# One decoder layer: the loads of the sample's cached sliding keys and values move from SyncE's queue to GpSimd's

## The chip, the cores and the metric

The kernel runs on one core of one Trainium2 chip, as one launch. The metric is the device time of that launch in microseconds (us), the median of several runs. Before the change it is 3061.63 us (three runs, 3060.77 to 3061.79).

TensorE (PE) multiplies matrices; its weight loads (PEld) are listed beside it. VectorE (DVE), ScalarE (ACT) and GpSimd (POOL) do elementwise work, and SyncE (SP) does none: it issues DMAs. Each engine takes its own instructions strictly in the order in which the program lists them, and an instruction waits for its semaphores with everything behind it.

## The reference, cut to what matters

One layer of a decoder trunk is computed for a prompt of 512 tokens and for a sample group of 8 sequences of 8 new tokens each, in float32. All 576 tokens share the weights. Four mixers (a gated delta rule, a state-space scan, a dilated sliding-window attention and a gated linear recurrence) feed one output projection, then follow cross-attention over 256 memory tokens and a convolved gated FFN.

The change touches only the sliding-window attention of the sample group. There each sequence has 2048 cached rows of keys and values, 8 heads of 64 channels:

```
k_ext = concatenate([k_buf, k_new], axis=1)          # v_ext likewise
for dist, bias in ((128, 1), (512, 4), (2048, 16)):  # (window, dilation)
    kg, vg = k_ext[:, lb + loc - dist], v_ext[:, lb + loc - dist]
    e = exp(q . kg * scale + bias - max);  out = sum(e * vg) / sum(e)
```

The 512 newest cached rows serve all three dilations. Of the 1536 older ones, only every sixteenth is read for a given query.

## The kernel before, in words

PE runs the projections as three passes (high by high, low by high, high by low halves) over weight blocks of 512 KB. `block` (L119) loads such a block into `raw` through SP; ACT and DVE split it into `hi` and `lo`; `linear` (L151) multiplies. All loads and stores of the program are issued by SP.

Nobody writes the order of an engine's instructions by hand. The program is traced with priorities, and a planner plays it forward in planned time, giving each engine its most urgent ready instruction; this fixes each engine's list. `at` sets the level: weights before drains, then "mix" (the delta rule among others), then "side", and "fill" last, at which `linear`'s matmuls are traced. The sample's attention is "side", called by `sample_step` from the callbacks of three projections: `swa_kv` (L856ff), `lru` and `delta_z`, while the delta rule (`delta`, L1411ff) is interleaved as "mix".

`sample_step` calls four parts, all of which the change touches through their loads:

- `old_keys(t0)`, for 8 query positions: six tiles of 128 rows by 512 (8 sequences, 16 old rows of each), loaded by `old` (L952), multiplied by the query (L967, four of six on POOL and two on DVE), and summed by head on DVE (L968).
- `old_values(t0)`: six such tiles of values (L952), weighted (L1012, again four of six on POOL) and added up on DVE (L1014).
- `sample_keys(pr, hp)`, 16 calls: two loads of 512 newest keys by 128 channels (L1054: each partition gets four runs of 512 bytes), which PE transposes (L1057); ACT or DVE copies the result, and PE forms the logits (L1063).
- `sample_values(pr)`, 4 calls: eight loads of 128 rows of values (L1095, 2 KB in each partition), which PE multiplies with the weights (L1100).

All of these loads are of 256 KB, and their tiles share four buffers (`tag="kn", bufs=4`). A load therefore waits until the tile four before it has been read for the last time. That last reader is POOL or DVE for an old tile, and PE for the newest keys and values.

POOL has other work in the same stretch: for the delta rule L1492, L1502, L1504, L1557, L1608, L1613 and L1636, and small copies at L869, L1070, L1298 and L1299. SP's queue holds, besides, the weight blocks (L119), the delta rule's inputs `dw<-dn` (L1459) and its sample states `dw<-in_state_delta` (L1606).

Of the kernel before, what the change touches and what calls it, by code (L numbers as in the profile page):

```python
# [284 lines left out]
class Post(Net):  # L285
    def add_x(self, g=None, first=False, out=False):

        nc = self.nc
        if g:
            self.xh, self.xl = {}, {}  # L290
            for k in range(15, -1, -1):
                self.xh[k], self.xl[k] = (self.xn[k // 4].tile([128, NT], F32R, name=f"x{z}{k}") for z in "hl")

        def done(m, ps):
            x = self.xT[:, m]
            with self.at("evac"):
                old = x
                if first:
                    old = self.nt()
                    nc.sync.dma_start(old, self.xd[m])  # L300
                nc.vector.tensor_tensor(x, ps, old, op=OP.add)  # L301
            if out:
                nc.sync.dma_start(self.xd[m], x)
            if g:
                nc.scalar.activation(self.xh[m], x, AF.Copy, scale=self.v(g, m))
                nc.vector.scalar_tensor_tensor(self.xl[m], x, self.v(g, m), self.xh[m], op0=OP.mult, op1=OP.subtract)
                if not out:
                    self.square(m)
        return done
# [484 lines left out]
class Swa(Post):  # L794
# [152 lines left out]
    def old(self, pool, name, k, t0):  # L947

        t = pool.tile([128, 512], F32, name="old", tag="kn", bufs=4)
        src = self.a[name]  # L950
        off = src[0, 0, 256 * k + t0, 0, 0:1].offset
        self.nc.sync.dma_start(t, bass.AP(tensor=src.tensor, offset=off, ap=[[2048 * 512, 8], [16 * 512, 16], [1, 512]]))  # L952
        return t

    def old_open(self, pool):
# [90 lines left out]
    def sample_keys(self, pr, hp):  # L1046

        nc, pool = self.nc, self.ok
        if hp == 0:
            self.S = pool.tile([128, 576], F32, name="S")  # L1050
        kt = []
        for b in (2 * pr, 2 * pr + 1):
            kn = pool.tile([128, 512], F32, name="kn", tag="kn", bufs=4).rearrange("p (j c) -> p j c", j=4)
            nc.sync.dma_start(kn, self.last("cache_win_k", b)[:, :, 128 * hp:128 * hp + 128])  # L1054
            p = self.pm()
            for j in range(4):
                nc.tensor.transpose(p[:, 128 * j:128 * j + 128], kn[:, j], self.ident)  # L1057
            kt.append(pool.tile([128, 512], F32, name="kt", tag="ow", bufs=2))
            (nc.scalar.copy if b % 2 else nc.vector.tensor_copy)(kt[-1], p)
        r = slice(32 * hp, 32 * hp + 32)  # L1060
        L = self.pm()
        for b2 in range(2):
            nc.tensor.matmul(L[r], self.Qm[:, hp, 2 * pr + b2], kt[b2], start=b2 == 0, stop=b2 == 1, skip_group_check=True)  # L1063
        nc.vector.tensor_tensor(self.S[r, :512], L[r], self.sb[r], op=OP.add)

    def sample_values(self, pr):

        nc, pool, S = self.nc, self.ok, self.S
        selh, sel2 = self.sel[:, :2], self.sel[:, 58:186].rearrange("p (g a b) -> p g a b", g=4, a=2)
        nc.gpsimd.tensor_copy(S[:, 512:], self.new[:, pr])  # L1070
        m, s = (pool.tile([128, 1], F32, name=f"sm{z}", bufs=2) for z in "ms")
        w = self.w4[:, pr:pr + 1]
        mo, so = self.mrow[:, 0, pr:pr + 1], self.mrow[:, 1, pr:pr + 1]
        nc.vector.tensor_reduce(m, S, axis=AX.X, op=OP.max, negate=True)
        nc.vector.tensor_tensor(m, m, mo, op=OP.min)
        nc.scalar.activation(S, S, AF.Exp, bias=m, accum_out=s)
        nc.scalar.activation(w, mo, AF.Exp, bias=m, scale=-1.0)
        nc.vector.scalar_tensor_tensor(s, so, w, s, op0=OP.mult, op1=OP.add)
        nc.vector.reciprocal(s, s)
        nc.vector.tensor_tensor(w, w, s, op=OP.mult)  # L1080
        pt = pool.tile([128, 512], F32, name="pt", tag="ow", bufs=2)
        p = self.pm()
        for j in range(4):
            nc.tensor.transpose(p[:, 128 * j:128 * j + 128], S[:, 128 * j:128 * j + 128], self.ident)
        nc.vector.tensor_copy(pt, p)
        p = self.pm()
        nc.tensor.transpose(p[:64, :128], S[:, 512:], self.ident)
        pn = S[:64, 256:384]
        nc.scalar.copy(pn, p[:64, :128])
        O = self.pm()  # L1090
        for b2 in range(2):
            for j in range(5):
                if j < 4:
                    v = pool.tile([128, 512], F32, name="v", tag="kn", bufs=4)
                    nc.sync.dma_start(v, self.last("cache_win_v", 2 * pr + b2)[:, j])  # L1095
                for hp in range(4):
                    c = slice(128 * hp, 128 * hp + 128)
                    r = slice(32 * hp, 32 * hp + 32)
                    lhs, rhs = (pt[:, 128 * j + 32 * hp:128 * j + 32 * hp + 32], v[:, c]) if j < 4 else (pn[:, r], self.vns[:, c])
                    nc.tensor.matmul(O[r, 128 * b2:128 * b2 + 128], lhs, rhs, start=j == 0, stop=j == 4, skip_group_check=True)  # L1100
        om = S[:, :256].rearrange("p (a e d) -> p a e d", a=2, e=2)
        for b2 in range(2):
            nc.vector.scalar_tensor_tensor(om[:, b2], O[:, 128 * b2:128 * b2 + 128].rearrange("p (e d) -> p e d", e=2), s,
                                           selh.unsqueeze(2).to_broadcast([128, 2, 64]), op0=OP.mult, op1=OP.mult)
        p = self.pm()
        for hp in range(4):
            for b2 in range(2):
                nc.tensor.matmul(p[:, 16 * hp:16 * hp + 16], om[:, b2].rearrange("p e d -> p (e d)"), sel2[:, hp, b2],
                                 start=hp == 0 and b2 == 0, stop=b2 == 1, skip_group_check=True)

        nc.vector.tensor_copy(self.kTs[:, :, 16 * pr:16 * pr + 16], p[:, :64].rearrange("p (a b) -> p a b", a=4))
# [1081 lines left out]
```

## Time and profile before

| | us |
|---|---|
| median of three runs | 3061.63 |
| the profiled execution's own time | 3060.31 |
| its span, first to last instruction | 3058.2 |
| PE busy | 2906.6 (95%) |
| DVE busy | 2083.6 (68%) |
| ACT busy | 1129.0 (37%) |
| POOL busy | 1098.4 (36%) |

The profiled execution lies 1.32 us under the median, and 2.1 us of it lie outside the span. DMA-issuing instructions are not counted as busy, so SP has no row. The first of the touched loads is issued 397.8 us after the start, the last one 991.4 us after it. The stretch from 380 to 1000 us is what the rows below mostly show.

### The profile page before, as it was taken

What the parts mean: (1) busy time and instruction counts of PE and PEld (TensorE: products, weight loads), DVE (VectorE), ACT (ScalarE), POOL (GpSimd) and SP (SyncE); (2) the same over time, 40 slices, a digit from 0 to 9 for tenths busy, and PEclk for the clock granted to TensorE, in tenths of its full rate; (3) what the DMA queues carried; (4) which work ended last, traced back from release to release, by engine and by line L of the source; (5) the groups of instructions that cost most, each with busy time, mean ns of one, the idle gap of its engine ahead of it and who ended that gap; (6) DMA issues with size and microseconds to landing.
All of it is one profiled execution on the core that took longest, in us unless ns stands there. A gap on an engine that the chain in (4) does not pass through costs nothing. (4 is left out here: it accounts for less than half of the span.)

```text
span 3058.2 us, 53977 instructions
## 1 busy us (share of the span) xinstructions
PE 2906.6 (95%) x21347; PEld 2743.7 (90%) x21347; DVE 2083.6 (68%) x3431; ACT 1129.0 (37%) x2013; POOL 1098.4 (36%) x1202
## 2 busy tenths in 40 slices
PE   8988988998999999998899999999999999999998
PEld 8888987887878879987889999999999999999996
DVE  7857756779567575648788888888888853333334
ACT  4433331353423353325344444444444432212214
POOL 4211422313112100102468889888888810000000
PEclk9999999999999999999999999999999999999999
DMA  5465566545576474244323333333333353333322
GB/s 169 133 192 152 163 181 187 166 130 163 166 209 181 136 216 143 68 127 151 118 88 110 107 102 109 107 103 110 106 100 105 113 201 114 101 97 114 107 90 104
DMA packets 370133, 408.41 MB, mean 134 GB/s; under 512 B 37718, under 2 KB 300715, under 8 KB 369176
## 3 DMA queue, kind: packets, MB, share of 16 engines
q1 hardware_dynamic: 369880, 404.96, 43.0%
q8 instruction: 168, 2.75, 0.4%
q14 instruction: 85, 0.70, 0.1%
HBM read 342.85 MB, written 64.69 MB: 133 GB/s over the span
## 5 line engine op out<-in xcount | busy, mean ns | idle before, releaser
L123 ACT CAST hi<-raw 128x1024 fp32r<-128x1024 f32 x158 | 165.6, 1048 | 489.9 <-PE acc L151 425.3
L151 PE MATMUL acc<-xh,hi 128*128 128x288 f32 x1408 | 319.3, 306 | 20.8 <-DVE nt L1192 13.8
L124 DVE TENSOR_TENSOR lo<-raw,hi 128x1024 fp32r<-128x1024 f32 x158 | 195.8, 1240 | 192.0 <-ACT hi L123 186.5
L151 PE MATMUL acc<-xh,lo 128*128 128x288 f32 x1408 | 317.8, 304 | 3.2 <-DVE lo L129 3.1
L151 PE MATMUL acc<-xl,hi 128*128 128x288 f32 x1408 | 317.5, 303 | 2.5 <-DVE xl L245 2.5
L344 DVE TENSOR_TENSOR lo<-S,hi 128x1024 fp32r<-128x1024 f32 x164 | 228.9, 1396 | 89.7 <-ACT hi L343 89.7
L151 PE MATMUL acc<-hh,hi 128*128 128x288 f32 x1280 | 276.1, 297 | 2.8 <-DVE xT L301 2.3
L151 PE MATMUL acc<-hh,lo 128*128 128x288 f32 x1280 | 274.3, 296 | 1.1 <-DVE lo L124 1.1
L151 PE MATMUL acc<-hl,hi 128*128 128x288 f32 x1280 | 275.0, 296 | 0.0
L344 DVE TENSOR_TENSOR al<-raw,ah 128x512 fp32r<-128x512 f32 x328 | 265.1, 844 | 14.2 <-ACT ah L343 14.1
L151 PEld LDWEIGHTS acc<-xh,hi 128*128 128x128 f32 x1408 | 231.8, 192 | 33.9 <-issue 26.6
L343 ACT CAST hi<-S 128x1024 fp32r<-128x1024 f32 x164 | 171.8, 1048 | 211.7 <-POOL S L539 176.9
L151 PEld LDWEIGHTS acc<-xl,hi 128*128 128x128 f32 x1408 | 232.7, 192 | 10.7 <-issue 7.4
L151 PEld LDWEIGHTS acc<-xh,lo 128*128 128x128 f32 x1408 | 231.6, 192 | 10.1 <-issue 4.6
L301 DVE TENSOR_TENSOR xT<-acc,xT 128x576 f32<-128x576 f32 x160 | 120.6, 755 | 168.3 <-PE acc L151 167.0
L536 POOL TENSOR_TENSOR S<-raw 128x256 f32<-128x256 f32 x164 | 168.8, 1029 | 154.5 <-DMA raw<-in_w_up 117.9
L128 ACT ACTIVATE hi<-raw,gmix 128x256 fp32r<-128x256 f32 x320 | 136.5, 498 | 212.8 <-PE acc L151 175.1
L151 PEld LDWEIGHTS acc<-hh,hi 128*128 128x128 f32 x1280 | 206.7, 189 | 3.6 <-ACT hi L123 2.2
L151 PEld LDWEIGHTS acc<-hh,lo 128*128 128x128 f32 x1280 | 207.0, 189 | 1.3 <-DVE lo L124 1.3
L151 PEld LDWEIGHTS acc<-hl,hi 128*128 128x128 f32 x1280 | 207.3, 189 | 0.0
L560 PE MATMUL acc<-Bh,ah 128*128 128x288 f32 x656 | 197.3, 301 | 10.3 <-ACT t L565 10.1
L634 DVE SCALAR_TENSOR_TENSOR y<-ub,vec,y 128x592 f32<-128x592 f32 x176 | 179.9, 1042 | 35.2 <-ACT y L632 34.4
(714 smaller groups left out, 8150.0 us busy)
## 6 DMA issues: line engine op xcount, KB each, us to landing
raw<-in_w_up SPq DMA_DIRECT2D x176, 512.0 KB
raw<-in_w_down SPq DMA_DIRECT2D x88, 512.0 KB
raw<-in_w_in SPq DMA_DIRECT2D x80, 512.0 KB
raw<-in_w_out SPq DMA_DIRECT2D x32, 512.0 KB
hx<-t SPq DMA_DIRECT2D x44, 288.0 KB
ht<-hx SPq DMA_DIRECT2D x44, 288.0 KB
old<-in_cache_win_k SPq DMA_DIRECT2D x48, 256.0 KB
old<-in_cache_win_v SPq DMA_DIRECT2D x48, 256.0 KB
```

The lines of the kernel that those rows point to most:

```text
L123: nc.scalar.copy(hi, raw)
L124: nc.vector.tensor_tensor(lo, raw, hi, op=OP.subtract)
L128: nc.scalar.activation(hi[:, k], raw[:, k], AF.Copy, scale=g)
L151: nc.tensor.matmul(acc[m][:, 224 + 288 * j:512 + 288 * j], wt[:, k, 128 * m:128 * m + 128], at(x, kb + k)[:, 288 * j:288 * j + 288], start ...
L301: nc.vector.tensor_tensor(x, ps, old, op=OP.add)
L343: self.nc.scalar.copy(hi, src)
L344: self.nc.vector.tensor_tensor(lo, src, hi, op=OP.subtract)
L536: g(S[:, 0], A(2, 1), A(2, 2), op=OP.add)
L560: nc.tensor.matmul(P[name], wt[:, i, q], xx, start=ch == chs[0] and q == 0 and j == 0, stop=ch == chs[3] and q == 1 and j == 2)
L634: nc.vector.scalar_tensor_tensor(y, u[:, k:k + 592], w(k), y, op0=OP.mult, op1=OP.add)
```

## The change

Three loads, in `old` (old keys and values), `sample_keys` and `sample_values`, are issued by `nc.gpsimd` instead of `nc.sync`. Their sources, tiles, buffers and levels stay as they are, and so does every computation. Each issue is now an instruction in POOL's list.

```diff
     def old(self, pool, name, k, t0):
...
-        self.nc.sync.dma_start(t, bass.AP(tensor=src.tensor, offset=off, ap=[[2048 * 512, 8], [16 * 512, 16], [1, 512]]))
+        self.nc.gpsimd.dma_start(t, bass.AP(tensor=src.tensor, offset=off, ap=[[2048 * 512, 8], [16 * 512, 16], [1, 512]]))
...
     def sample_keys(self, pr, hp):
...
-            nc.sync.dma_start(kn, self.last("cache_win_k", b)[:, :, 128 * hp:128 * hp + 128])
+            nc.gpsimd.dma_start(kn, self.last("cache_win_k", b)[:, :, 128 * hp:128 * hp + 128])
...
     def sample_values(self, pr):
...
-                    nc.sync.dma_start(v, self.last("cache_win_v", 2 * pr + b2)[:, j])
+                    nc.gpsimd.dma_start(v, self.last("cache_win_v", 2 * pr + b2)[:, j])
```

## Rows read from the trace of the kernel before

**Rows 1.** The page's head: span, and busy time of each engine.

```profile
span 3058.2 us, 53977 instructions
PE 2906.6 (95%) x21347; PEld 2743.7 (90%) x21347; DVE 2083.6 (68%) x3431; ACT 1129.0 (37%) x2013; POOL 1098.4 (36%) x1202
```

**Rows 2.** Busy us of each engine in the stretch; then clock, DMA share, GB/s.

```profile
380.00:1000.00 620.00, 567.69 (x4299) 498.61 (x4299) 430.26 (x805) 210.63 (x460) 151.13 (x146) 0.97 0.60 174
```

**Rows 3.** PE's waits from 380 to 1000 us: total us, times, longest.

```profile
PE pm L1462 <- DMA dw<-dn: 8.7, 5, 4.3
PE pm L1057 <- DMA kn<-in_cache_win_k: 7.5, 5, 3.8
PE pm L1479 <- DVE dw L1473: 4.6, 1, 4.6
PE pm L1100 <- DMA v<-in_cache_win_v: 4.5, 7, 2.3
PE ov L1618 <- DMA dw<-in_state_delta: 2.0, 2, 1.6
PE ov L1618 <- POOL dw L1613: 1.7, 1, 1.7
```

**Rows 4.** The page's DMA queues: packets, MB, share of 16 engines.

```profile
q1 hardware_dynamic: 369880, 404.96, 43.0%
```

**Rows 5.** The touched issues: count, ns least/median/most, first and last start.

```profile
L952 SPq DMA_DIRECT2D old<-in_cache_win_k x48: 596/612/2226, 397.8 to 598.3; - x48
L952 SPq DMA_DIRECT2D old<-in_cache_win_v x48: 596/609/1209, 670.8 to 954.6; - x48
L1054 SPq DMA_DIRECT2D kn<-in_cache_win_k x32: 366/373/1607, 482.5 to 956.6; - x32
L1095 SPq DMA_DIRECT2D v<-in_cache_win_v x32: 327/360/1154, 603.5 to 991.4; - x32
```

**Rows 6.** SP's waits in the same stretch: weight blocks, then the touched lines' largest.

```profile
SPq L119 <- DVE lo L129: 49.2, 18, 15.5
SPq L952 <- POOL ow L1012: 26.7, 15, 6.1
SPq L952 <- PE pm L1057: 11.7, 8, 4.3
SPq L952 <- POOL ow L967: 11.3, 8, 4.4
SPq L1095 <- PE pm L1057: 10.0, 6, 3.6
SPq L1095 <- PE pm L1100: 9.9, 6, 4.9
SPq L1054 <- DVE ow L1012: 9.9, 5, 4.1
SPq L952 <- DMA old<-in_cache_win_v: 9.8, 4, 4.0
SPq L952 <- PE acc L151: 8.9, 4, 6.4
```

**Rows 7.** POOL's groups: count, ns least/median/most, first and last start.

```profile
L967 POOL TENSOR_TENSOR ow<-old,q x32: 1263/1292/1812, 407.0 to 604.9; 128x512 f32<-128x512 f32 x32
L1557 POOL TENSOR_TENSOR dw<-dw,dm x16: 1261/1291/2271, 584.1 to 1003.6; 128x512 f32<-128x512 f32 x16
```

**Rows 8.** POOL's waits in the stretch: two of the largest.

```profile
POOL dw L1636 <- ACT dw L1634: 74.3, 4, 26.8
POOL ow L1012 <- PE pm L1063: 53.1, 5, 15.2
```

**Rows 9.** SP in order of time: the last batch of newest values.

```profile
990.01 1.76 SPq L1095 DMA_DIRECT2D v<-in_cache_win_v  x4
```

**Rows 10.** When the sample's result is stored for the output projection.

```profile
L1141 SPq DMA_DIRECT2D mixT<-kTs x1: 420/420/420, 1072.5 to 1072.5; - x1
L2019 SPq DMA_DIRECT2D nt<-mixT x16: 319/381/569, 805.2 to 1196.8; - x16
```

## The prediction, made before the changed kernel ran

> **What bounds the kernel now.** I read the page's head first. PE is busy 2906.6 us of a span of 3058.2, and no other engine is above 68% [rows 1]. The end is therefore set by PE's work plus the time in which PE stands idle, 151.6 us in all. The change adds and removes no PE instruction, so it can move the time only by moving idle time of PE. Next I read the busy times by stretch. From 380 to 1000 us, in which every touched load is issued [rows 5], PE is busy 567.7 of 620 us: 52.3 us are idle there, and POOL is busy 151.1 [rows 2]. What is outside that stretch neither loses nor gains a touched instruction.
>
> Third, I read who ended PE's waits in it [rows 3]. The reader is to see two kinds of DMA. PE waited 12 times, 12.0 us together, for touched loads (7.5 us for the newest keys, 4.5 for the newest values). It waited 7 times, 10.7 us together, for loads that stay on SP (8.7 and 2.0 us, both the delta rule's inputs). It waited for POOL once, 1.7 us. The rest of the idle time is mostly single waits for DVE, of which the largest stands in [rows 3].
>
> Last come the queues. All program DMAs now run through one hardware queue [rows 4], and no DMA issued by POOL stands anywhere in the trace. SP is held up a lot at the touched lines: their eight largest entries make 98.2 us, 38.0 of them because POOL had not yet read the buffer's old contents [rows 6].
>
> **What leaves SP.** It loses 96 + 32 + 32 = 160 issues: 48 x 0.612 + 48 x 0.609 + 32 x 0.373 + 32 x 0.360 = 82 us by the medians [rows 5], and the 98.2 us and more of waits [rows 6] behind which other loads stood. Weight blocks gain nothing that PE feels, since none of PE's larger waits there is for a weight block. What can be late because of SP are the two loads named above, 10.7 us. Between none of it and all of it I take two thirds, **-7 us**: the largest wait on SP that stays is that of the weight blocks for their own buffers, 49.2 us, and the touched lines' 98.2 are two thirds of the two together [rows 6].
>
> **What POOL gets: the price of an issue.** It is in no row. From below, the nearest row is SP's issue of the same transfer, 0.36 us [rows 5]. From above it is POOL's own operation over a tile of the same shape, 128 by 512, at 1.29 us [rows 7]. Nothing excludes more, since the newest keys are fetched in four runs per partition and so in four times as many pieces (a rival, below). I take 1.29, because an issue in POOL's list is POOL's work, and its row for this tile is nearer than another engine's. That makes 160 x 1.29 = 206 us more in POOL's list; with 151.1 it holds 357 of 620 us.
>
> **Loads that arrive later at PE.** The newest keys come in pairs. By the chosen price the first of a pair is late by 1.29 - 0.37 = 0.9 us and the second by twice that, 1.8 us, 1.4 in the mean. For values it is steeper: SP issues a batch of four in 1.76 us [rows 9], and POOL would take 4 x 1.29 = 5.2. I charge only the places where PE already waits today, for there is no slack there: 12 waits [rows 3] x 1.4 = **+17 us**. At SP's price this is 0. The other 52 loads arrive before they are needed, and what covers their lateness is that PE has matmuls of the running projection in between; the planner redraws PE's list around the new landings, which covers part of it if it foresees them. Without that cover the batches alone would cost 4 x (5.2 - 1.76) = 14 us more, once for the second batch of each `sample_values`, whose buffers are freed only by the first.
>
> **Work behind a waiting issue on POOL.** An issue still needs its buffer. Of the 98.2 us that SP waited, POOL's own reads (38.0 us) vanish as waits, because they then stand earlier in the same list. The other 60 us, on PE, DVE and earlier DMAs, now stop POOL. Queued behind them are the multiplications of old tiles, for which DVE waits, and the delta rule's POOL operations, for which PE's delta matmuls wait in the end. POOL would be held 357 + 60 = 417 of 620 us, two thirds. Most of its delta work is wanted late: PE waited for POOL once in the whole stretch [rows 3], and POOL itself stood 74.3 us waiting for the delta rule's gate and 53.1 for PE [rows 8], so it is early and not late. I charge three late arrivals of the size of that one wait, 3 x 1.7 = **+5 us**; at SP's price none.
>
> **The sum.** -7 + 17 + 5 = +15 us. On the profiled execution's 3060.3 us this gives 3075.3; that execution lies 1.3 us under the median of the runs, so I forecast 3061.6 + 15 = 3076.6, rounded 3077. The sample's result does not become the next bound: it is stored at 1072.5 us, and the output projection is still fetching its inputs at 1196.8 [rows 10].
>
> One rule of the Trainium skill is set against this. The trace shows 82 us of issue time leaving SP [rows 5]. The Trainium skill, "DMA: Bandwidth & Descriptors", section "Issuing engines are not separate DMA queues", says that DMAs from SP and from GpSimd run on the same 16 engines and interleave, and that issuing from several engines saves only the sequencer's time. The same page, "Latency and other measured facts", gives about 0.6 us to the first byte from SP and about 1 us from GpSimd. An estimate from that page: 0.4 us more at each of 12 waits is 5 us in place of 17, and the sum -7 + 5 + 5 = +3. That would be no change that can be told; no run so far shows a GpSimd issue.
>
> **Rivals.**
>
> *Nothing to see.* The planner puts PE's transposes where the loads land in its plan, and projection matmuls fill the time between, so what POOL adds stays hidden. For it: 52 of 64 loads of newest rows make PE wait for nothing today [rows 3, 5]. Against it: PE's list is fixed beforehand, and each microsecond by which a load lands after its planned time is idle time. It gives -7 + 5, so 3060, within 6 us of now.
>
> *Faster: SP's queue was what made the inputs late.* The place is SP's list, where touched loads waiting for buffers hold up everything behind them. If POOL's issue costs no more than SP's, the first term comes whole and the touched loads no longer queue behind weight blocks: 10.7 + 12.0 = 22.7 us at most [rows 3]; half of it gives 3061.6 - 11 = 3050. It decides from the price: between 0.36 and 1.29 us the second and third terms go from 0 to 22, so they stay under the 7 of the first below 0.36 + 0.93 x 7 / 22 = 0.66 us. For it: 98 us of SP waits at these lines [rows 6]. Against it: PE felt only 22.7 us of all this.
>
> *Much slower: the newest keys cost by the piece.* With four runs in each partition, an issue at L1054 would be 4 x 1.29 = 5.2 us and a pair 10.3. First and second are then late by 4.8 and 9.6 us. The five waits at L1057 [rows 3] grow by 7.2 in the mean, 36 us, in place of their 7 us share of the 17; POOL's list grows by 32 x 3.9 = 124 us to 481 of 620 before any wait, which makes its delta work late at, say, ten more places of 1.7 us, 17 us. Sum 15 + 29 + 17 = +61, so 3123.
>
> That the loads don't move is not to be expected; the queue rows will tell.
>
> **How the numbers follow.** Forecast (clearly slower, up to some 45 us) 0.38; much slower 0.11; nothing to see 0.25; faster 0.26. A change within 0.2%, 6 us, cannot be told from none in this kernel. So faster 0.26, same 0.25, slower 0.49. The forecast's own range is 3068 to 3107. The range for 8 in 10 reaches from 3045, just under the faster rival, to 3113, which leaves out the upper half of the much slower one: cases of both signs hold the chance, and the unknown price from 0.36 to 1.29 us and beyond makes it this wide.
>
> **What would show it.** In the profile after: a second, software queue with 160 x 256 KB = 42 MB; issue rows on POOL, whose duration is the price (1.29 wanted, 0.36 for the faster rival, several times more at L1054 than at L1095 for the much slower one). PE's waits at L1057 and L1100 should grow from 12 us to some 29, those for the delta rule's inputs fall from 10.7 to about 4, and those for POOL rise from 1.7 to about 7. PE's idle time in the stretch should rise from 52 to about 67 us. The prediction is wrong if the added idle time lies outside 380 to 1000 us, or if it is ended by something that I do not charge, DVE first of all.

## The result and the profile after

The kernel after takes 3082.66 us (median of four runs, 3081.09 to 3085.87) against 3061.71 for the kernel before on the same chip. The ratio is 1.0066, with an interval of 1.0053 to 1.0079: 21 us slower, where +15 was forecast. The loads moved as the diff says. First, the page of the kernel after: its head [rows 1] and two DMA queues (packets, MB, share of 16 engines) [rows 4].

```profile
span 3081.3 us, 53957 instructions
PE 2918.7 (95%) x21347; PEld 2758.9 (90%) x21347; DVE 2098.1 (68%) x3431; ACT 1128.0 (37%) x2013; POOL 1186.4 (39%) x1362
...
q1 hardware_dynamic: 335320, 363.01, 38.5%
q0 software_dynamic: 18944, 42.00, 5.3%
```

The touched issues (count, ns least/median/most, first and last start) [rows 5]:

```profile
L952 POOL DMA_DIRECT2D old<-in_cache_win_k x48: 584/623/806, 395.5 to 608.1; - x48
L952 POOL DMA_DIRECT2D old<-in_cache_win_v x48: 584/620/802, 682.2 to 994.0; - x48
L1054 POOL DMA_DIRECT2D kn<-in_cache_win_k x32: 747/801/843, 493.3 to 996.3; - x32
L1095 POOL DMA_DIRECT2D v<-in_cache_win_v x32: 537/547/592, 615.9 to 1028.2; - x32
```

The software queue carries 42 MB, as expected. An issue costs POOL 0.55 to 0.80 us. The span has grown by 23.1 us: PE is busy 12.1 us longer with the same 21347 matmuls, and idle 11.0 us longer. Where, the stretches tell (columns as in [rows 2]). The kernel before, in the stretch from 1000 us on:

```profile
1000.00:1300.00 300.00, 296.59 (x1958) 262.84 (x1957) 185.19 (x333) 126.98 (x234) 23.31 (x18) 1.00 0.45 140
```

The kernel after, in both stretches:

```profile
380.00:1000.00 620.00, 563.96 (x4182) 501.15 (x4181) 435.40 (x786) 208.37 (x453) 237.77 (x295) 0.96 0.63 169
1000.00:1300.00 300.00, 287.46 (x1942) 255.70 (x1941) 185.75 (x330) 122.87 (x226) 30.17 (x30) 0.98 0.48 148
```

In the stretch of the touched loads PE is idle for 56.0 us, only 3.7 more than before [rows 2]. From 1000 to 1300, where only the last eight of these loads remain, it is idle for 12.5 us where it was 3.4. The granted clock is lower in both. PE's waits in the two stretches of the kernel after (total us, times, longest; the largest of each, and the only one for POOL):

```profile
PE pm L1462 <- DMA dw<-dn: 10.2, 5, 4.2
PE pm L1532 <- DVE dw L1558: 6.6, 3, 2.6
...
PE ov L1618 <- POOL dw L1613: 2.7, 2, 2.3
...
PE kp L363 <- DMA km<-in_cache_mem_k: 6.4, 1, 6.4
PE pm L180 <- DMA nt<-in_mem_prompt: 5.1, 1, 5.1
```

No wait for a newest key or value is left (12.0 us before [rows 3]), and the two large new ones stand in code that the change doesn't touch. The first of them, at L363 (memory keys), can be followed: SP issues its loads only behind the store of the prompt attention's last heads (L945).

```profile
1213.70 0.34 SPq L945 DMA_DIRECT2D mixT<-ob  x1
...
1216.09 1.97 SPq L360 DMA_DIRECT2D km<-in_cache_mem_k  x4
```

In the kernel before, these loads are issued from 1178.2 us on, and no wait follows. The prompt's attention in turn is late because the sample is. The matmuls at L1108, which close each pair's part of the sample's attention (count, ns least/median/most, first and last start), before and after:

```profile
L1108 PE MATMUL pm<-sel,S x64: 177/263/263, 687.4 to 1004.4; 128*128 128x16 f32 x64
```

```profile
L1108 PE MATMUL pm<-sel,S x64: 177/263/263, 687.4 to 1041.9; 128*128 128x16 f32 x64
```

Both start at 687.4 us; the last one has moved from 1004.4 to 1041.9. PSUM, where PE puts its results, has banks. The prompt's attention uses banks 2 and 3 from its second group of heads on, and the sample uses bank 2, so the two take turns: the second group's first logits go from 1007.2 to 1045.2, the last matmul of the whole prompt attention from 1175 to 1213, and the last part of the output projection, which needs that attention, ends at 1271.5 in place of 1250.0. In PE's list itself, the last of L1108 stands behind 4445 of the projections' matmuls (L151) before and 4612 after; some texts below call this the place of the sample's last logits. So there were two theories: **LIST**, that the planner's new order of PE's list is the loss (LATENESS in four of the texts below), and **PRICE**, that the GpSimd issues cost the time on the chip.

### The profile page after: what moved, and what is told of

Same layout as the page of the kernel before. It is cut to its first block, busy times and chain, and to the rows that moved or that the text cites. A ratio compares the mean times of both kernels' runs of the same rounds, so it can differ in the third digit from the quotient of the medians.

```text
span 3081.3 us, 53957 instructions
## 1 busy us (share of the span) xinstructions
PE 2918.7 (95%) x21347; PEld 2758.9 (90%) x21347; DVE 2098.1 (68%) x3431; ACT 1128.0 (37%) x2013; POOL 1186.4 (39%) x1362
## 5 line engine op out<-in xcount | busy, mean ns | idle before, releaser
L151 PE MATMUL acc<-xh,hi 128*128 128x288 f32 x1408 | 321.7, 309 | 24.6 <-DVE nt L1192 16.3
L151 PE MATMUL acc<-xh,lo 128*128 128x288 f32 x1408 | 322.8, 308 | 3.7 <-DVE lo L129 3.6
L151 PE MATMUL acc<-xl,hi 128*128 128x288 f32 x1408 | 322.4, 307 | 2.5 <-DVE xl L245 2.5
L151 PE MATMUL acc<-hh,hi 128*128 128x288 f32 x1280 | 275.5, 297 | 2.2 <-DVE xT L301 1.7
L151 PE MATMUL acc<-hh,lo 128*128 128x288 f32 x1280 | 274.1, 296 | 1.1 <-DVE lo L124 1.1
L151 PE MATMUL acc<-hl,hi 128*128 128x288 f32 x1280 | 274.6, 296 | 0.0
L151 PEld LDWEIGHTS acc<-xh,hi 128*128 128x128 f32 x1408 | 235.9, 196 | 35.3 <-issue 23.8
L151 PEld LDWEIGHTS acc<-xh,lo 128*128 128x128 f32 x1408 | 235.9, 195 | 12.6 <-issue 6.8
L151 PEld LDWEIGHTS acc<-xl,hi 128*128 128x128 f32 x1408 | 237.2, 196 | 10.9 <-issue 6.9
L151 PEld LDWEIGHTS acc<-hh,hi 128*128 128x128 f32 x1280 | 206.1, 188 | 2.9 <-ACT hi L123 1.6
L151 PEld LDWEIGHTS acc<-hh,lo 128*128 128x128 f32 x1280 | 206.6, 188 | 1.3 <-DVE lo L124 1.3
L151 PEld LDWEIGHTS acc<-hl,hi 128*128 128x128 f32 x1280 | 206.7, 188 | 0.0
L560 PE MATMUL pp<-Th,hi 128*128 128x288 f32 x656 | 195.8, 301 | 8.7 <-DVE u L570 4.3
```

The lines of the kernel that those rows point to most:

```text
L151: nc.tensor.matmul(acc[m][:, 224 + 288 * j:512 + 288 * j], wt[:, k, 128 * m:128 * m + 128], at(x, kb + k)[:, 288 * j:288 * j + 288], start ...
L560: nc.tensor.matmul(P[name], wt[:, i, q], xx, start=ch == chs[0] and q == 0 and j == 0, stop=ch == chs[3] and q == 1 and j == 2)
```

## The experiments

Each ratio is against the kernel before on the same chip; its median was 3059.97 to 3063.02 us. A single profiled execution can lie almost 10 us from its kernel's median (run 1: 3061.81 us against 3071.36), so verdicts go by the ratios.

**1 and 2. One part alone.** Old loads alone on GpSimd; newest loads alone.

The first:

```diff
-        self.nc.sync.dma_start(t, bass.AP(tensor=src.tensor, offset=off, ap=[[2048 * 512, 8], [16 * 512, 16], [1, 512]]))
+        self.nc.gpsimd.dma_start(t, bass.AP(tensor=src.tensor, offset=off, ap=[[2048 * 512, 8], [16 * 512, 16], [1, 512]]))
```

The second:

```diff
-            nc.sync.dma_start(kn, self.last("cache_win_k", b)[:, :, 128 * hp:128 * hp + 128])
+            nc.gpsimd.dma_start(kn, self.last("cache_win_k", b)[:, :, 128 * hp:128 * hp + 128])
...
-                    nc.sync.dma_start(v, self.last("cache_win_v", 2 * pr + b2)[:, j])
+                    nc.gpsimd.dma_start(v, self.last("cache_win_v", 2 * pr + b2)[:, j])
```

> Only the 96 loads of old keys and values (L952) are issued by GpSimd; the newest keys and values stay on SyncE. Theory LIST: the loss is made in the planner's lists. PE's list holds the sample's last matmul (L1108) behind 4445 projection matmuls before the change, behind 4612 after it, and here behind 4571; the prompt's attention, which takes turns with the sample on one PSUM bank, ends (L942) behind 4935, 5124 and here 5031, while the projection that needs it starts behind 5090 in all three. Here it ends before that start, so the second half of the loss (about 13 us) should be missing and the first (about 8) should be there in part: 3064 to 3072 us. Rival PRICE: each issue on GpSimd costs time on the chip. The old loads are 59 of the 102 us that the 160 issues took, so 59/102 of 21 us: 3074 us.

> Only the 64 loads of the newest keys and values (L1054, L1095) are issued by GpSimd. Theory LIST: the sample's last matmul stands behind 4671 projection matmuls, later than in the full change (4612), and the prompt's attention ends behind 5079, hardly ahead of 5090: most of the loss should be there although only two fifths of the loads moved, 3072 to 3083 us. Rival PRICE: 43 of 102 us of issue time, 3070 us.

Measured: 3071.36 us, 1.0029 (1.0014 to 1.0043), and 3090.96 us, 1.0086 (1.0062 to 1.0111). The first parts nothing: it lies in LIST's range, and PRICE's 3074 us lies in its interval. The 64 newest loads alone cost no less than all 160 (the intervals overlap), 21 us more than PRICE gave them, and no price per issue can give that; the last sample matmuls of that kernel ended at 1063.5 us, later than in any other. LIST had the sign but put the second too low.

**3 and 4. The sample and the prompt's attention on banks of their own,** on the kernel after and on the kernel before.

```diff
-            self.banks = (3,) if hp < 1 else (2, 3)
+            self.banks = (3,) if hp < 1 else (1, 3)
```

> The changed kernel, but the prompt's attention takes its PSUM tiles from banks 1 and 3 instead of 2 and 3, so that it no longer takes turns with the sample (bank 2). Theory LIST: all 160 GpSimd issues and the late sample (4612) stay, but the prompt's attention now ends behind 4704 projection matmuls. The second half of the loss goes: 3062 to 3071 us. Rival PRICE: all issues are still on GpSimd, so all of the loss stays: 3078 to 3086 us.

> Control for the third run: the kernel before with the same banks 1 and 3 for the prompt's attention (all loads on SyncE). Theory LIST: the sample ends behind 4445 as before and the prompt's attention behind 4704; before, nothing waited on it, so 3055 to 3064 us, and the changed kernel with these banks stays within 10 us of it. Rival PRICE: the same 3055 to 3064 here, but 21 us less than the third run.

Measured: 3118.24 us, 1.0174 (1.0146 to 1.0202), and 3112.74 us, 1.0166 (1.013 to 1.0201). Both theories missed the level: the memory keys' projection uses bank 1 as well and could start only at 1141.1 and 1136.9 us, behind the prompt's attention. The pair is of use all the same. With this common wait, which the sample doesn't enter, the whole change, issues and new lists, costs 5.5 us, and the intervals overlap, so it may as well be nothing.

**5 and 8. Lateness without any GpSimd issue.** Three buffers in place of four, for all five tiles of the tag, make the sample late (the first diff); bank 3 alone makes the prompt's attention late with the sample on time (the second).

```diff
-        t = pool.tile([128, 512], F32, name="old", tag="kn", bufs=4)
+        t = pool.tile([128, 512], F32, name="old", tag="kn", bufs=3)
```

```diff
-            self.banks = (3,) if hp < 1 else (2, 3)
+            self.banks = (3,)
```

> The kernel before, every load on SyncE as it was, with three buffers in place of four for the touched tiles. Nothing is issued by GpSimd, but the loads must wait longer for their buffers, and PE's list puts the last of the sample's logits at place 4592 of the projection's matmuls (before 4445, after 4612). LATENESS (PE's list has the sample later, and bank 2 of PSUM hands that on to the prompt's attention and to the last part of the output projection): the sample's last matmuls end near 1035 to 1042 us, the projection's last part near 1268 us (before 1250), 3070 to 3085 us. PRICE (each GpSimd issue costs time): no such issue, 3060 to 3065.

> The kernel before, loads on SyncE, with the prompt's attention on PSUM bank 3 alone to its end. The sample is as early as before (place 4435 of its last logits), but the prompt's attention, with one bank in place of two, ends late in PE's list, at place 5124 as in the kernel after (before 4935). LATENESS says that the end of the prompt's attention is what counts, whatever made it late: the output projection's last part ends near 1265 us, 3068 to 3080. PRICE: no GpSimd issue, 3058 to 3065.

Measured: 3091.91 us, 1.0092 (1.0076 to 1.0108), and 3093.49 us, 1.0093 (1.0074 to 1.0112): 28 us each, more than LIST asked for. In the second, PE from 1000 to 1300 us:

```profile
1000.00:1300.00 300.00, 274.56 (x1744) 239.88 (x1743) 173.27 (x293) 116.63 (x209) 22.35 (x16) 0.94 0.44 133
```

25.4 us are idle there, and the clock is 0.94. Of the idle time, 10.0 us are waits inside the prompt's attention (L937 for DVE), which has one bank here, and 6.9 us the wait at L363. So a prompt attention that ends late (1221.7 us) can cost what the change costs, without any GpSimd issue. It does not yet say that it did.

**6 and 7. The link loosened without touching bank 1.** The prompt's attention keeps to bank 3 for its first two groups, on the kernel after and on the kernel before.

```diff
-            self.banks = (3,) if hp < 1 else (2, 3)
+            self.banks = (3,) if hp < 2 else (2, 3)
```

> The kernel after, all 160 loads on GpSimd, with the prompt's attention kept on PSUM bank 3 alone for its first two groups of heads in place of the first one, so that its second group doesn't take turns with the sample on bank 2. The places in PE's list: sample's last logits 4606 (as after), prompt attention's last matmul 4853 (after 5124). LATENESS: the prompt's attention ends before 1170 us (after 1213), the output projection's last part no longer waits for it, and most of the loss goes: 3058 to 3070 us. PRICE: the 160 issues are all there, 3078 to 3086.

> The kernel before, loads on SyncE, with the same change of banks as the run on the kernel after (bank 3 alone for two groups). Places: sample's last logits 4435, prompt attention's last matmul 4914. It is the control: what the banks alone are worth. LATENESS: the prompt's attention ends about where it did (4935 before), 3055 to 3064, and the kernel after with these banks lies at most 8 us above this one. PRICE: 3055 to 3064 too, and the kernel after with these banks lies some 21 us above this one.

Measured: 3080.7 us, 1.0058 (1.0043 to 1.0073), and 3056.28 us, 0.9978 (0.9966 to 0.9989). The second is faster than both kernels. But the first didn't recover: the prompt's attention ended at 1181.3 us, 32 us earlier than in the kernel after if not before 1170, PE was idle for only 5.5 us from 1000 to 1300, and the loss stayed. LIST, as the whole cause, fell here, and PRICE's 21 us came back as 24.

**9 and 10. The exchange.** To part the two causes, the kernel is planned twice. The first plan's lists of PE, ScalarE and VectorE are then held, instruction for instruction, in the second, where the loads are issued by the other engine. The ties only order an engine's own list and add no wait between engines.

```diff
-            nc.sync.dma_start(kn, self.last("cache_win_k", b)[:, :, 128 * hp:128 * hp + 128])
+            self.issuer.dma_start(kn, self.last("cache_win_k", b)[:, :, 128 * hp:128 * hp + 128])
...
+PINNED = ("PE", "Activation", "DVE")
...
+                behind = mybir.DependencyInfo(mybir.DependencyClass.NoSync, mybir.DependencyReason.DATA)
+                for names in lists:
+                    for one, two in zip(names, names[1:]):
+                        tc.add_manual_dep(byname[two], one, behind, reason="list")
...
+    _, lists = build("sync")
+    nc, kept = build("gpsimd", lists)
```

(The tenth has the last two engines the other way round.)

> All 160 loads issued by GpSimd as in the kernel after, but the lists of PE, ScalarE and VectorE are held instruction for instruction to those that the planner made for the kernel before (the last of the sample's logits at place 4445, the prompt attention's last matmul at 4935); only the lists of GpSimd and SyncE are laid out anew. LIST (the loss is in the order of PE's list): nearly all of the loss is gone, 3058 to 3068 us, the sample's last matmul ends within 8 us of 1004.7. PRICE (the loss is what GpSimd's issues and the waits behind them cost on the chip): it stays or grows, since PE's list now expects the loads earlier, 3078 to 3095 us, with PE waiting for touched loads at L1057 and L1100 well over the 12.0 us of before.

> The other half of the exchange: every load issued by SyncE as in the kernel before, but the lists of PE, ScalarE and VectorE held to those of the kernel after (places 4612 and 5124). No GpSimd issue at all. LIST: the loss is all there, 3076 to 3088 us, the output projection's last part ends near 1270 us (before 1250.0). PRICE: no loss, 3058 to 3066 us.

| lists of PE, ACT, DVE | loads issued by SyncE | loads issued by GpSimd |
|---|---|---|
| those of before | 1 (the kernel before) | 1.0056 (1.0043 to 1.0069), 3079.41 us |
| those of after | 1.0029 (1.0017 to 1.0041), 3072.54 us | 1.0066 (1.0053 to 1.0079), the kernel after, on another chip |

Both causes are real. The issues alone cost 0.56%, 17 us; the new lists alone 0.29%, 9 us. Together they cost 21 and not 26, so in the lists made for them the issues cost 0.37%, 11 us; but each ratio has an interval of 0.12 to 0.13% to either side, and these 5 us are not clear of it. LIST missed the ninth by 11 us and the tenth by 3.5; PRICE had the ninth's time, and missed the tenth by 6.5. The end of the output projection's last part tells the causes apart in neither: it is 1272.1 us in the ninth, as late as in the kernel after, and 1257.9 in the tenth, not near 1270.

The traces of the ninth kernel and of the kernel before have PE's 21347 matmuls in the same order. So one can look for each lost microsecond between the same two instructions. The ninth's profiled execution is the slowest of its five (3084.5 us, 5 above the median), so the division below is that execution's, which took 24 us longer than the profiled one before. The same 3911 matmuls, first before, then in the ninth (columns as in [rows 2]):

```profile
390.01:960.06 570.05, 518.43 (x3911) 455.44 (x3910) 401.21 (x756) 195.97 (x435) 145.91 (x141) 0.97 0.60 173
```

```profile
389.63:980.73 591.10, 531.77 (x3911) 468.91 (x3910) 406.15 (x754) 195.73 (x435) 233.18 (x293) 0.94 0.62 167
```

They take 21.1 us longer, which is all that this execution lost up to there, and most of its 24; before 390 us the two agree within 0.4 us. Idle time is only 7.7 us of it (51.6 to 59.3). The other 13.3 are the same matmuls taking longer, at a mean clock of 0.94 instead of 0.97: 0.03 of 591 is 18 us by the rounded means. In the clock's records the lower level, 1.2 GHz, holds for 34 us from 380 to 1000 before, 55 in the kernel after and 68 in the ninth. The slower clock isn't that one execution's: the mean granted clock is 0.978 to 0.980 in the ninth's five executions and 0.981 to 0.985 in the eleven of the kernel before beside them. The idle part is made of many small waits. Some of the ninth's from 380 to 1000 us, to be set beside [rows 3]:

```profile
PE pm L1057 <- DMA kn<-in_cache_win_k: 12.3, 7, 4.8
PE pm L1462 <- DMA dw<-dn: 9.5, 4, 4.1
PE pm L879 <- DVE nt L874: 6.6, 2, 4.2
...
PE pm L1100 <- DMA v<-in_cache_win_v: 4.5, 6, 1.8
```

Touched loads make PE wait for 16.8 us (12.0 before), SP's delta inputs for 9.5 (10.7), VectorE for 29.2 by all its rows (25.0), ScalarE for 4.1 (2.3), POOL not at all (1.7). One of these shows a way by which POOL's list reaches PE. The ninth kernel in order of time (start, us, engine, line):

```profile
690.53 1.17 POOL L952 DMA_DIRECT2D old<-in_cache_win_v  x2 [2.73 <-DVE acc L1012]
691.71 1.08 POOL L1012 TENSOR_TENSOR ow<-old,lo 128x512 f32<-128x512 f32 x1
692.73 1.28 POOL L1492 TENSOR_TENSOR qg<-dw 128x512 f32<-128x512 f32 x1
...
694.09 1.06 POOL L1012 TENSOR_TENSOR ow<-old,lo 128x512 f32<-128x512 f32 x1
...
692.83 3.43 DVE L1014 TENSOR_TENSOR acc<-acc,ow 128x512 f32<-128x512 f32 x1 [2.59 <-POOL ow L1012]
696.18 0.68 DVE L1496 TENSOR_TENSOR dw<-pm,gc 128x512 f32<-128x512 f32 x1
...
696.91 2.08 PE L1514 MATMUL pm<-dw 128*128 128x128 f32 x8 [3.43 <-DVE dw L1496]
```

PE in that kernel right after this (stretch, its length, busy us and matmuls, then clock, DMA share, GB/s):

```profile
697.00:707.00 10.00, 10.00 (x45) 0.50 0.43 118
707.00:712.00 5.00, 5.00 (x41) 1.00 0.93 265
```

The same three steps in the kernel before:

```profile
681.22 0.69 DVE L1014 TENSOR_TENSOR acc<-acc,ow 128x512 f32<-128x512 f32 x1 [3.39 <-POOL ow L1012]
681.83 0.68 DVE L1496 TENSOR_TENSOR dw<-pm,gc 128x512 f32<-128x512 f32 x1
...
686.55 1.05 PE L1514 MATMUL pm<-dw 128*128 128x128 f32 x8
```

POOL issues two loads, multiplies, and goes straight on. VectorE's addition beside it takes 3.43 us in place of 0.69; the delta rule's product behind it on VectorE is late; PE stands for 3.43 us; and then the clock is at its lower level until 707: 45 matmuls take 10 us where 41 take 5 right after it. So some 5 us more go on half speed behind a wait of 3.4 us. But the kernel before has a stall of its own just ahead of these steps, a wait for newest values with the lower clock behind it (a matmul group in order of time, then a stretch as in [rows 2]):

```profile
676.48 0.43 PE L1100 MATMUL pm<-v,pt 128*32 128x128 f32 x8 [2.26 <-DMA v<-in_cache_win_v]
677.00:684.00 7.00, 6.71 (x37) 5.02 (x38) 2.81 (x6) 0.60 (x1) 2.59 (x3) 0.51 0.65 196
```

From the matmul at 615.7 us to the one at 715.3 (628.3 and 727.8 in the ninth) both kernels take 99.5 us. The passage shows a way, then, and no net loss. Right behind it stands a wait that does count, first in the ninth (with a stretch of PE as above), then before:

```profile
735.95 1.05 PE L1532 MATMUL pm<-dw 128*128 128x128 f32 x8
738.01 0.82 POOL L1054 DMA_DIRECT2D kn<-in_cache_win_k  x1
744.01 1.09 PE L1057 MATMUL pm<-ident,kn 128*128 128x128 f32 x4 [4.84 <-DMA kn<-in_cache_win_k]
741.00:748.00 7.00, 3.99 (x18) 0.51 0.81 179
```

```profile
721.65 4.95 SPq L1054 DMA_DIRECT2D kn<-in_cache_win_k  x2
723.37 1.05 PE L1532 MATMUL pm<-dw 128*128 128x128 f32 x8
727.41 0.63 PE L1057 MATMUL pm<-ident,kn 128*128 128x128 f32 x4 [0.83 <-DVE lo L129]
```

SP had issued this load 1.7 us ahead of PE's L1532; POOL, busy with a multiplication and two old loads, issues it 2.1 us after. PE waits 4.84 us in place of 0.83, and the clock falls. From L1532 to the same matmul of L151 (729.45 before, 747.77 in the ninth) PE takes 11.8 us instead of 6.1. The clock's record also has falls at other places in both kernels: the rows show falls that follow waits, and no run here gives the one without the other.

**11. The held lists with the other banks.** The same exchange on the kernel of run 7 (diffs as in 7 and 9).

> All 160 loads issued by GpSimd, with the lists of PE, ScalarE and VectorE held to those of the kernel before with PSUM bank 3 alone for the prompt attention's first two groups (that kernel, loads on SyncE, took 3056.28 us; the kernel after with the same banks 3080.70, which LIST had put at 3058 to 3070). It tells whether the 24 us between those two are the list again or GpSimd's issues. LIST: 3052 to 3062 us. PRICE: 3075 to 3090 us.

Measured: 3076.18 us, 1.0044 (1.003 to 1.0058), against 0.9978 for the same lists with SyncE: the issues cost 0.66%, 20 us. That is PRICE's range, and it settles run 6: most of its 24 us are the issues again.

**12. Old loads alone, lists held.**

As in run 9, but with the newest loads left on SyncE:

```diff
-            self.issuer.dma_start(kn, self.last("cache_win_k", b)[:, :, 128 * hp:128 * hp + 128])
+            nc.sync.dma_start(kn, self.last("cache_win_k", b)[:, :, 128 * hp:128 * hp + 128])
...
-                    self.issuer.dma_start(v, self.last("cache_win_v", 2 * pr + b2)[:, j])
+                    nc.sync.dma_start(v, self.last("cache_win_v", 2 * pr + b2)[:, j])
```

> The lists of PE, ScalarE and VectorE held to those of the kernel before, and only the 96 old keys and values issued by GpSimd; the 64 newest loads stay on SyncE. With all 160 on GpSimd and the same lists it was 3079.41 us, +16.7. BY ISSUE (the price goes with GpSimd's issue time, of which the old loads are 59 of 102 us): about 10 us of it, 3070 to 3077. BY NEWEST KEYS (the price starts at PE's own waits for the newest keys, 12.3 us with all on GpSimd against 7.5 before): those waits stay near 7.5 us and the time comes back, 3060 to 3067. In either case I expect more time at half clock from 380 to 1000 us where PE is idle more: idle and half-clock time go up or down together.

Measured: 3072.11 us, 1.0042 (1.0028 to 1.0056). The share by issue was right (+12 to 13 us), and the newest keys are not the only start: PE waits 6.1 us for them here. The interval overlaps that of run 9, so how the price divides between old and newest loads stays open. In its profile the same 3911 matmuls take 5.0 us longer, at 0.96; idle time is 1.4 us of it and slower matmuls 3.6, so both went up, as expected:

```profile
390.07:965.16 575.09, 522.05 (x3911) 462.83 (x3909) 409.67 (x757) 196.12 (x435) 197.80 (x237) 0.96 0.63 172
```

That execution, 3066.9 us, is the lowest of its five.

## Why the prediction was right, and where its steps failed

The sign and the size held: +21 us against +15, with a forecast whose own range began at 3068. The mechanism held in part for one of two causes, the issues; the other, the new lists, was not in the sum, and several terms were wrong.

*"What bounds the kernel now"* held in that no engine took PE's place. It went on that the change "can move the time only by moving idle time of PE", and that failed: half of the loss is in neither added work nor idle time, since PE is busy 12.1 us longer with the same matmuls. **The step that failed first is the one that costs an idle microsecond at one microsecond.** In the held lists 7.7 us of idle time came with 13.3 us of slower matmuls.

*The price of an issue, 1.29 us,* was too high: 0.55 to 0.80, mean 103 us / 160 = 0.64. The upper end of the bounds was a POOL computation, which an issue isn't; and the lower end, 0.36, left out that 96 of the 160 issues took SP 0.61 [rows 5], so that SP's own mean was 82 / 160 = 0.51. The Trainium skill, "SBUF — State Buffer", section "SBUF: two separate sides", warns that some VectorE operations keep GpSimd from writing a DMA's descriptors, so that the transfer waits. No row here shows that: the longest of the 160 issues took 0.843 us, and how long a transfer waited for its descriptors no row tells. The same section says that VectorE and GpSimd share one pair of ports as an exclusive lock, and that a VectorE operation with two SBUF inputs can be the one that is locked out. L1014 has two such inputs, and its 3.43 us beside POOL's operations agree with that; no run here takes it by itself.

*The much slower rival,* the newest keys by the piece, is refuted in its size: with four runs in each partition L1054 takes 0.80 us, not 5.2. That is 1.3 to 1.5 times what the other touched loads take.

*The faster rival* was to decide from 0.66 us, and the mean price, 0.64, lies on its side; it still didn't come. What failed is the term it rested on, **"What leaves SP", -7 us**: PE's waits for the two delta inputs went from 10.7 us to 11.2 in the kernel after, and to 9.5 with the lists held, -1.2. The waits on SP were real, but taking them away did not bring those inputs in earlier; what makes them late stays open.

*Loads that arrive later, +17 us.* In the kernel after these waits fell from 12.0 us to none. The text named the reason, that "the planner redraws PE's list around the new landings, which covers part of it if it foresees them", and then didn't price it. The planner's new lists cover all of it by setting the sample's work later, and these lists cost 9 us by themselves (run 10). With the lists held, the term measures +4.8 us of waits.

*Work behind a waiting issue on POOL, +5 us.* POOL stood 183 us before the touched issues in the kernel after, where the text had 60, and still PE's wait for POOL only went from 1.7 to 2.7 us, and to none with the lists held. PE's waits for VectorE rose by 4.2 us with the lists held; that what POOL delays reaches PE this way is shown for one of them (3.43 us, run 9), and not for the rest. The text itself had named waits ended by DVE as a sign of being wrong. *Nothing to see* is ruled out by the interval of the ratio. So is the +3 us of the estimate from the Trainium skill's "DMA: Bandwidth & Descriptors", section "Latency and other measured facts": with the lists held the issues cost 17 us, and no run here measured the first byte alone.

*"The sample's result does not become the next bound"* was wrong. I looked at its stored result, which is still early (1083.6 us), and not at what else its lateness holds: PSUM bank 2, behind which the prompt's attention and the output projection's last part stand. By the text's own test, that it is wrong if the added idle time lies outside 380 to 1000 us, it failed for the kernel as built: 3.7 us lie inside and 9.1 from 1000 to 1300. Runs 9 and 10 show that this second part belongs to the lists: with those of before PE is idle for 4.2 us there although GpSimd issues the loads. Run 10, with no GpSimd issue at all:

```profile
380.00:1000.00 620.00, 570.49 (x4315) 508.81 (x4314) 424.89 (x803) 212.32 (x461) 156.90 (x149) 0.97 0.59 174
1000.00:1300.00 300.00, 286.80 (x1932) 252.58 (x1931) 181.24 (x331) 124.51 (x234) 23.66 (x18) 0.98 0.46 143
```

Up to 1000 us PE is idle for 49.5 us, less than before; from 1000 to 1300 for 13.2, which is 9.8 more. This execution is the fastest of its seven (3067.18 us) and took 7 us longer than the profiled one before, with PE busy 2.0 us less; by the medians the run cost 9. Where the other six lost more is not shown; their mean clock is 0.978 to 0.980, this one's 0.981.

So the sum -7 + 17 + 5 came near 21 with its two large terms far off. What the runs put in its place, in the slowest execution with the lists held: -1.2 (SP's inputs), +4.8 (touched loads), +4.2 (VectorE), -1.7 (POOL), +1.8 (ScalarE), together 7.9 by the rows for 7.7 us of idle time, and 13.3 us of slower matmuls; and in the kernel as built, 9 us for the order of the lists less what that order saves. The sign follows from late loads, which the text had. That the size came out near the forecast is luck.

Left open: why the change cost some 5 us, or nothing, where a common wait follows (runs 3 and 4) and 21 without it is argued from that wait, not shown; in run 2 the loss was not parted into lists and issues; and no run held the lists without exchanging the engine, so what the second planning does by itself to the lists of GpSimd and SyncE is not measured. Nor is the issue parted from the transfer: the software queue's 42 MB take 5.3% of the DMA engines' span where the hardware queue's share fell by 4.5. In the one wait followed above the later issue (3.8 us) covers nearly all of the longer wait (4.0).

## What to carry to other kernels

Where a planner lays out the lists, a change of one instruction's engine is two changes: what the chip does with it, and another order for everything else. Part them by holding the lists and exchanging only the engine; without that, either cause could here be made to look like the whole. When PE is the bound and its clock has two levels, price a short stall by the clock behind it too. And look for lateness in every resource that the late work holds (here a PSUM bank), not only in its result.

## What the runs showed that was not expected

- A plain 256 KB load costs GpSimd 0.55 to 0.62 us to issue with one run per partition and 0.80 with four; SP took 0.36 to 0.61 [rows 5].
- Beside POOL's operations the same VectorE addition (L1014) took up to 3.8 us in the ninth kernel and up to 1.8 in the kernel before, where its medians are 0.69 and 0.68. None of those that ran beside no POOL instruction (10 of 40 and 27 of 40) took over 0.70.
- Keeping the prompt's attention on one PSUM bank for two groups of heads rather than one, with SyncE issuing, is worth 0.22% (0.11 to 0.34): 3056.28 us, the fastest version here.
